# First stage of a one-core hybrid attention step: root, doubled rows, transposes, dummies and channel share changed

## The chip, the core and the metric

The kernel runs on one core of a Trainium2 chip. The metric is the device time of one execution, in microseconds (us). The engines are TensorE (PE for its matmuls, PEld for its weight loads), VectorE (DVE), ScalarE (ACT), GpSimd (POOL) and SyncE (SP, which issues most DMAs).

## What is computed

One layer of a decoder step, for 1024 prompt tokens and 8 sample tokens of width 1024. The input is normalised by its root mean square and multiplied with one combined weight; the columns of the result feed a gated short convolution and an attention with three branches (compressed, selected, window). Cut to what the change touches:

```
def rms_norm(x, g):
    xf = xf * lax.rsqrt(jnp.mean(xf * xf, axis=-1, keepdims=True) + NORM_EPS)
    return (xf * g.astype(jnp.float32)).astype(x.dtype)
...
    h = rms_norm(x, norm_g)
    proj = h @ w_in
    b_gate, c_gate, conv_in, z_conv, q, kv, gate_logits, z_attn = jnp.split(proj, offs, axis=-1)
    q = rope(rms_norm(q, q_gain), pos) * (HEAD_DIM ** -0.5)
    k = rope(rms_norm(kv[:, :, :, 0], k_gain[:, None, :]), pos)
...
    attn_branch = attn_o.reshape(bsz, t, ATTN_W) * jax.nn.silu(z_attn)
```

## The kernel before, in words

Every fp32 product is made of halves: an operand is split into a high part (a copy rounded to fp32r, on ACT) and a low part (the difference, on DVE or POOL), and three matmuls are added up in one PSUM bank. `w_loader` (L152) fetches weight pieces by DMA into `wraw` buffers and splits them into `wh` and `wl`; `wl0` serves the token products (256 or 280 columns, two `wraw` buffers), `w1` the channel products (128 weight columns).

The first stage is `phase0` (L519). It goes over 9 token tiles (8 of 128 prompt tokens, one of 8 sample tokens) five times, once per weight: the key/value rows of the compressed branch (`c0`), of the selected branch (`c1`), of the window branch (`c2`), and the queries in two halves. `tok_mm` (L193) makes one product of a tile: 24 matmuls into one of three `mm` banks.

`x_norm` (L368) prepares an input tile two tiles ahead: sum of squares on ACT, `rsqrt` (L180), scaling on DVE (L374), eight transposes on PE (L380), and the split into `hH` (ACT) and `hL` (DVE). `rsqrt` computes mean plus epsilon on DVE (L184), the root on ACT (L185), and four DVE instructions that take the reciprocal and mend it by one step. `norm_rope` (L245) does the same per head for key and query rows: squares (two heads by two ACT instructions with a running sum, L251; four heads by one ACT instruction and a DVE reduction, L253 and L254), `rsqrt`, and rope on DVE (L258 to L266).

Key rows must stand doubled before they are transposed. `twice` (L268) copies them on DVE into a `kd` tile; the tile for four rows shares one buffer with other small things (`CWR`), that for two rows has one buffer. `post` (L490) keeps the transposes that follow (`cmp_transposes` L390, `k_finish` L474) back by one step; `twice` is called there, together with them.

Beside `phase0` runs a second stream of products, `chan_stream` (L306): four weight columns of 128 for the attention's gate (`z_attn`), three products each (384, 384 and 264 tokens, 24 matmuls each, L215 to L217), copied into `mixA`. `merge` (L30) decides which stream goes next: always the one with the smaller ratio of work done to its weight, 150 for `phase0` and `ZW` = 31 for the channel stream; the numbers that the streams yield are their work. When both are done, one ACT instruction applies SiLU to the whole of `mixA` (L642), and attention begins; the later channel products belong to the convolution and fill attention's gaps.

The order on each engine is not that of the code: a scheduler sorts the recorded instructions, and each engine then takes them strictly in turn. So the printed order decides what queues behind what.

## Time and profile before

| | us |
|---|---|
| median of 3 runs (lowest, highest) | 952.64 (951.82, 954.2) |
| the profiled execution | 951.0 |
| its span, first to last instruction | 948.9 |
| PE busy | 876.9 (92%), 5765 matmuls |
| DVE busy | 612.6 (65%) |
| ACT busy | 556.1 (59%) |
| POOL busy | 404.1 (43%) |

The span is what the trace covers; the profiled execution is 2.1 us longer, the runs' median 1.6 us more than that. Times in the trace count from the start of the span. A busy PE can still be slow: its clock has two levels, 2.4 GHz (granted clock 1.00) and 1.2 GHz (0.50).

### The profile page before, as it was taken

The numbers are of one execution on the slowest core, as the hardware profiler recorded it, in microseconds if no ns is written. First come the engines' busy times: TensorE is split into PE (matmuls) and PEld (weight loads), VectorE is DVE, ScalarE is ACT, GpSimd is POOL, SyncE is SP. The second block draws the span as 40 slices with busy tenths as digits, with TensorE's granted clock in tenths as the row PEclk, the third lists the DMA queues.
The fourth block names the chain that finished last, engine by engine and source line by source line (L and its number), as shares of the span: only waits on it lengthen the run. The fifth ranks groups of instructions, "written<-read, shape, count | busy, mean of one in ns | idle before, by whom it ended". The sixth has DMA issues, their size and how long they took to land.

```text
span 948.9 us, 16963 instructions
## 1 busy us (share of the span) xinstructions
PE 876.9 (92%) x5765; PEld 787.1 (83%) x5765; DVE 612.6 (65%) x1744; ACT 556.1 (59%) x1489; POOL 404.1 (43%) x550
## 2 busy tenths in 40 slices
PE   5989889999999999999999999999779999798998
PEld 4878879899879889998998998999668888576765
DVE  3887656588456555567557558547845555777883
ACT  5754434533668667565656555555846766676761
POOL 4213322221366543444444443342364543467761
PEclk9999989999999999999999999999979999799999
DMA  6614230311000000000000000000477562847631
GB/s 220 176 35 114 65 121 24 90 56 31 23 24 22 13 12 23 23 23 23 25 23 23 23 23 23 22 2 1 118 260 264 188 203 82 309 148 252 202 110 46
DMA packets 57954, 82.23 MB, mean 87 GB/s; under 512 B 14470, under 2 KB 43086, under 8 KB 55692
## 3 DMA queue, kind: packets, MB, share of 16 engines
q1 hardware_dynamic: 50956, 47.60, 16.7%
q0 software_dynamic: 6912, 33.56, 10.5%
q8 instruction: 45, 0.74, 0.3%
q14 instruction: 41, 0.34, 0.1%
HBM read 74.24 MB, written 11.10 MB: 90 GB/s over the span
## 4 chain that ended last, share of the span: by engine, by line
PE 46%; DVE 6%; ACT 6%; issue 3%; DMA 2%; POOL 2%; SPq 0%; ACTq 0%; POOLq 0%; DVEq 0%
PE o L845 6%; PE mm L217 5%; PE mm L216 5%; PE mm L215 5%; PE s L762 5%; PE pt L836 4%; PE pt L956 1%; PE mm L1364 1%; PE mm L1362 1%; PE mm L1363 1%; PE o L1235 1%; PE om L980 1%; PE mm L980 1%; PE pt L1163 1%; ACT P L752 1%
## 5 line engine op out<-in xcount | busy, mean ns | idle before, releaser
L215 PE MATMUL mm<-hH,wh 128*128 128x384 f32 (+1 forms) x480 | 159.1, 331 | 0.0
L216 PE MATMUL mm<-hL,wh 128*128 128x384 f32 (+1 forms) x480 | 156.6, 326 | 0.0
L217 PE MATMUL mm<-hH,wl 128*128 128x384 f32 (+1 forms) x480 | 156.2, 326 | 0.2 <-POOL wl L78 0.2
L78 POOL TENSOR_TENSOR wl<-wraw,wh 128x256 fp32r<-128x256 f32 (+1 forms) x120 | 90.8, 774 | 120.4 <-ACT wh L74 89.7
L752 ACT ACTIVATE P<-P,stat 128x640 f32<-128x640 f32 (+7 forms) x192 | 113.0, 590 | 43.0 <-DVE stat L750 42.2
L78 DVE TENSOR_TENSOR pl<-pt,ph 128x512 fp32r<-128x512 f32 (+1 forms) x164 | 101.8, 634 | 45.6 <-ACT ph L74 44.6
L74 ACT ACTIVATE ph<-pt 128x512 fp32r<-128x512 f32 (+1 forms) x164 | 87.1, 547 | 57.5 <-PE pt L836 56.6
L811 POOL TENSOR_SCALAR P<-P,stat,gates 128x640 f32<-128x640 f32 (+7 forms) x128 | 101.3, 800 | 42.9 <-DVE stat L802 34.6
L836 PE MATMUL pt<-ident,P 128*128 128x128 f32 x592 | 93.3, 279 | 6.5 <-POOL P L811 2.1
L762 PE MATMUL s<-k,q 128*128 128x320 f32 (+8 forms) x416 | 96.4, 335 | 2.0 <-ACT q L74 1.9
L200 PE MATMUL mm<-wh,hH 128*128 128x256 f32 (+1 forms) x320 | 95.2, 299 | 2.9 <-ACT wh L74 1.9
L201 PE MATMUL mm<-wl,hH 128*128 128x256 f32 (+1 forms) x320 | 95.7, 299 | 1.5 <-POOL wl L78 1.0
L202 PE MATMUL mm<-wh,hL 128*128 128x256 f32 (+1 forms) x320 | 94.8, 297 | 0.4 <-DVE hL L78 0.2
L217 PEld LDWEIGHTS mm<-hH,wl 128*128 128x128 f32 x480 | 92.5, 193 | 0.6 <-POOL wl L78 0.5
L215 PEld LDWEIGHTS mm<-hH,wh 128*128 128x128 f32 x480 | 92.7, 193 | 0.3 <-ACT wh L74 0.2
L216 PEld LDWEIGHTS mm<-hL,wh 128*128 128x128 f32 x480 | 92.6, 193 | 0.1
L750 DVE CUSTOM_DVE_ANT_0 P<-s,mask 128x32 f32<-128x32 f32 (+8 forms) x160 | 69.8, 473 | 34.2 <-PE s L762 28.5
L836 PEld LDWEIGHTS pt<-ident,P 128*128 128x128 f32 x592 | 69.7, 141 | 18.1 <-POOL P L811 7.5
L845 PE MATMUL o<-pl,v 128*128 128x256 f32 x264 | 73.4, 300 | 5.6 <-DVE pl L78 5.4
L845 PE MATMUL o<-ph,v 128*128 128x256 f32 x264 | 74.8, 301 | 2.9 <-ACT ph L74 2.5
L762 PEld LDWEIGHTS s<-k,q 128*128 128x128 f32 x416 | 67.0, 191 | 5.8 <-ACT q L74 2.5
L807 POOL TENSOR_SCALAR P<-P,stat,gates 128x32 f32<-128x32 f32 x64 | 22.7, 367 | 108.5 <-DVE stat L802 97.4
(339 smaller groups left out, 2177.7 us busy)
## 6 DMA issues: line engine op xcount, KB each, us to landing
wraw<-in_w_in_dram SPq DMA_DIRECT2D x56, 256.0 KB
xt<-in_x_prompt_dram SPq DMA_DIRECT2D x8, 512.0 KB
wor<-in_w_out_dram SPq DMA_DIRECT2D x16, 256.0 KB
xr<-in_x_prompt_dram SPq DMA_DIRECT2D x16, 256.0 KB
out_y_prompt_dram<-xr SPq DMA_DIRECT2D x16, 256.0 KB
sd<-in_state_win_kv_dram SPq DMA_DIRECT2D x8, 512.0 KB
out_s_win_dram<-in_state_win_kv_dram SPq DMA_DIRECT2D x8, 511.0 KB
cwr<-in_cmp_w_dram SPq DMA_DIRECT2D x32, 64.0 KB
```

What stands on the lines that cost most here:

```text
L78: return eng.tensor_tensor(out, a, b, OP.subtract)
L200: PE.matmul(o[:, :n], hH[t // 3][:, k, s], wh, start=k == 0, stop=False)
L201: PE.matmul(o[:, :n], hH[t // 3][:, k, s], wl, start=False, stop=False)
L202: PE.matmul(o[:, :n], hL[t // 3][:, k, s], wh, start=False, stop=k == 7)
L215: PE.matmul(o[:, :n], wh, hH[c][:, k], start=k == 0, stop=False)
L216: PE.matmul(o[:, :n], wh, hL[c][:, k], start=False, stop=False)
L217: PE.matmul(o[:, :n], wl, hH[c][:, k], start=False, stop=k == 7)
L752: return lambda: ACT.activation(P, P, AF.Exp, bias=stt[:, 0, c:c + 1], scale=-1.0, accum_out=stt[:, 1, c:c + 1])
L762: PE.matmul(s[:, a:b], q[:, i], k, start=first, stop=not first)
L811: POOL.tensor_scalar(P[:, i, :n], P[:, i, :n], stt[:, 2, c + i:c + i + 1], gates[:, qi, gt:gt + 1], op0=OP.mult, op1=OP.mult)
L836: PE.transpose(p[:, y * 256 + i * 128:y * 256 + i * 128 + 128], src[:, i], ident)
L845: PE.matmul(o[0][:, :256], v, X[:, y * 256:y * 256 + 256], start=br == 1 and x == 0 and y == 0 and X is h[0], stop=last and y + 1 == len(p ...
```

## The change

- `rsqrt` takes the sum of squares already divided: ACT's square gets the scale 1/32 (inputs) or 1/8 (heads). The root is taken of the mean directly, with epsilon as the bias of the ACT instruction; the first DVE instruction (L184) goes. A root of a constant is issued at the start.
- The queries' sums come from four ACT squares per tile with running sums; the DVE reduction (L254) goes.
- 24 dummy matmuls with an operand of zeros are issued at the start. They write a bank that a later product overwrites.
- The third and fourth piece of the first weight get buffers of their own in the input tiles' pool.
- `x_norm` returns its transposes; they are called behind the next tile's product. `twice` is called as soon as the rows are made; `posted` lets the transposes follow after one step (`cmp_transposes`) or two (`k_finish`). The tile for two rows has three buffers instead of one, `rows` three instead of four.
- `ZW` goes from 31 to 55; SiLU on `mixA` is issued when the channel stream's four columns are done. The compression weight's split follows its fetch by one tile, and the second weight's splits follow their fetches by one tile.

```
+    WARM = 24
...
+    eps = cst.tile([128, 2], F32, name="eps")
+    DVE.memset(eps, EPS)
+    eps, root = eps[:, 0:1], eps[:, 1:2]
+    ACT.activation(root, eps, AF.Sqrt)
...
+    warm = ps.tile([128, 512], F32, name="cc", tag="cc", bufs=2)
+    for _ in range(WARM):
+        PE.matmul(warm[:, :256], vpc[:, 0], vpc.rearrange("p g c -> p (g c)"), start=True, stop=True)
...
+            def fetch(i, home=wp):
+                r = home.tile([128, kp, n], F32, name="wraw", bufs=raw_bufs)
                 SP.dma_start(r[:, :, :width], w_in[:, i * kp:(i + 1) * kp, col:col + width])
...
-    def rsqrt(wk, ss, n, c, scale):
-
-        t = wk.tile([128, 4, 8], F32, name="rs", bufs=4)
-        v, s, r, a = (t[:n, i, :c] for i in range(4))
-        DVE.tensor_scalar(v, ss, scale, EPS, op0=OP.mult, op1=OP.add)
-        ACT.activation(s, v, AF.Sqrt)
+    def rsqrt(wk, ss, n, c):
+
+        t = wk.tile([128, 3, 8], F32, name="rs", bufs=4)
+        s, r, a = (t[:n, i, :c] for i in range(3))
+        ACT.activation(s, ss, AF.Sqrt, bias=eps[:n])
         DVE.reciprocal(r, s)
-        DVE.tensor_tensor(a, v, r, OP.mult)
+        DVE.scalar_tensor_tensor(a, ss, EPS, r, op0=OP.add, op1=OP.mult)
         DVE.scalar_tensor_tensor(a, a, -0.5, r, op0=OP.mult, op1=OP.mult)
         DVE.scalar_tensor_tensor(r, a, 1.5, r, op0=OP.add, op1=OP.mult)
...
-        if nh == 2:
-            for h in range(2):
-                ACT.activation(sq[:n, h * 64:h * 64 + 64], src[:, h * 64:h * 64 + 64], AF.Square, accum_out=ss[:n, h:h + 1])
-        else:
-            ACT.activation(sq[:n, :w], src, AF.Square)
-            DVE.tensor_reduce(ss[:n, :nh], sq[:n, :w].rearrange("p (h d) -> p h d", h=nh), axis=AX, op=OP.add)
-        r = rsqrt(wk, ss[:n, :nh], n, nh, 1.0 / 64)
+        for h in range(nh):
+            c = slice(h * 64, h * 64 + 64)
+            ACT.activation(sq[:n, c], src[:, c], AF.Square, scale=0.125, accum_out=ss[:n, h:h + 1])
+        r = rsqrt(wk, ss[:n, :nh], n, nh)
...
-        kd = wk.tile([128, n, 2, 64], F32, name=f"kd{n}", tag="cwr" if n == 4 else "kd2", bufs=CWR if n == 4 else 1)
+        kd = wk.tile([128, n, 2, 64], F32, name=f"kd{n}", tag="cwr" if n == 4 else "kd2", bufs=CWR if n == 4 else 3)
...
-    LAG, DEPTH, HK, HB, XB, ZW, CWR = 1, 2, 2, 4, 3, 31.0, 1
+    LAG, DEPTH, HK, HB, XB, ZW, CWR = 1, 2, 2, 4, 3, 55.0, 1
...
-    ROWS, KLAG, CLAG = 4, 1, 1
+    ROWS = 3
...
     def x_norm(t):
...
-        ACT.activation(junk[:n], xt, AF.Square, accum_out=ss[:n])
-        r = rsqrt(wk, ss[:n], n, 1, 1.0 / D)
+        ACT.activation(junk[:n], xt, AF.Square, scale=1.0 / 32, accum_out=ss[:n])
+        r = rsqrt(wk, ss[:n], n, 1)
         DVE.scalar_tensor_tensor(xt, xt, r, gbc[:n], op0=OP.mult, op1=OP.mult)
-        for b in range(2):
...
+        def turn_x():
+            for b in range(2):
+                p = bank("tp")
...
+            seen[0] = t + 1
+        return turn_x
+
+    def cmp_transposes(kd, t):
+
...
-    def k_finish(br, t, rows2):
+    def k_finish(br, t, kds):

         p = bank("tp")
         pv = p.rearrange("p (g c) -> p g c", g=2)
         for i in range(2):
-            kd = twice(wk, rows2[i], 2)
             for g in range(2):
-                PE.transpose(pv[:, g, i * 128:i * 128 + 128], kd[:, g].rearrange("p r d -> p (r d)"), ident)
+                PE.transpose(pv[:, g, i * 128:i * 128 + 128], kds[i][:, g].rearrange("p r d -> p (r d)"), ident)
...
-    def post(fn, lag):
-
-        posts.append(fn)
-        while len(posts) > lag:
-            posts.pop(0)()
+    def posted(steps):
+
+        posts[:] = [(fn, n - steps) for fn, n in posts]
+        while posts and posts[0][1] <= 0:
+            posts.pop(0)[0]()

     def kv_tile(t, w, n, br, tab):
-        rows, _ = kv_rows(wk, tok_mm(t, w, n), t, br, *tab)
+        o = tok_mm(t, w, n)
+        posted(1)
+        rows, _ = kv_rows(wk, o, t, br, *tab)
         if t < 8:
             v = V[br][:, t]
             rv = rows[:, 128:256].rearrange("p (g d) -> p g d", g=2)
             copy(ACT, v[:, :, 0:64], rv)
             sub(POOL, v[:, :, 64:128], rv, f(v[:, :, 0:64]))
-            late[br].append(rows)
+            late[br].append(twice(wk, rows, 2))
         if t in (1, 3, 5, 7):
-            post(lambda r=late[br], t=t: k_finish(br, t - 1, r), KLAG)
+            posts.append((lambda r=late[br], t=t: k_finish(br, t - 1, r), 2))
             late[br] = []

...
+        posted(1)
...
         x_load(1)
-        c0[1](2)
+        c0[1](2, xsp)
+        c0[1](3, xsp)
         x_load(2)
         SP.dma_start(rope0, io["c_rope"])
-        x_norm(0)
+        turns = [x_norm(0)]
+        turns.pop(0)()
         tab0 = rope_tables(io["k_gain"][0, 0], 0, 1.0)
         for i in range(4):
             c0[2](i, *E0)
-            if i == 0:
-                c0[1](3)
         x_load(3)
-        x_norm(1)
+        turns.append(x_norm(1))
+        turns.pop(0)()
         c1 = wl0(COL_KV + 256, 256)
         for t in range(NT):
             if t + 4 < NT:
                 x_load(t + 4)
             if t + 2 < NT:
-                x_norm(t + 2)
-            rows, _ = kv_rows(wk, tok_mm(t, c0[0], 256), t, 0, *tab0)
+                turns.append(x_norm(t + 2))
+            o = tok_mm(t, c0[0], 256)
+            if turns:
+                turns.pop(0)()
+            posted(1)
+            rows, _ = kv_rows(wk, o, t, 0, *tab0)
             if t < 8:
-                post(lambda rows=rows, t=t: cmp_transposes(rows, t), CLAG)
+                posts.append((lambda kd=twice(wk, rows, 4), t=t: cmp_transposes(kd, t), 1))
             if t == 7:
                 tab1 = rope_tables(io["k_gain"][0, 1], 1, 1.0)
+            if t in (1, 2):
+                for i in (2 * t - 2, 2 * t - 1):
+                    c1[2](i)
             if t < 2:
                 for i in (2 * t, 2 * t + 1):
                     c1[1](i)
...
+        posted(9)
         xss.close()
         cw = xcp2.enter_context(pool("cw")).tile([128, 16, 2, 128], F32R, name="cw")
-        post(lambda: None, 0)
...
+            if 0 < t < 5:
+                cw_split()
             if t < 4:
-                cw_piece(wk, cw, t)
+                cw_split = cw_fetch(wk, cw, t)
             yield 3400
...
             yield next(chan)
+        ACT.activation(mAf, mAf, AF.Silu)

     merge((phase0(), 150.0), (z_part(), ZW))
-    ACT.activation(mAf, mAf, AF.Silu)
```

How the printed order moves, in three places. First PE, where the first weight's first products stand (`tp<-ident,xt` are the transposes of an input tile, `mm` the product). Before:

```order
L202 MATMUL mm_244<-wh_172,hL0_89 128x256
L200 MATMUL mm_244<-wh_176,hH0_88 128x256
L201 MATMUL mm_244<-wl_177,hH0_88 128x256
L380 MATMUL tp_204<-ident_58,xt_122 128x128 x4
L380 MATMUL tp_211<-ident_58,xt_122 128x128 x4
L202 MATMUL mm_244<-wh_176,hL0_89 128x256
L200 MATMUL mm_244<-wh_180,hH0_88 128x256
```

And after the change:

```order
L209 MATMUL mm_255<-wl_216,hH0_91 128x256
L210 MATMUL mm_255<-wh_215,hL0_92 128x256
L388 MATMUL tp_230<-ident_58,xt_150 128x128 x4
L388 MATMUL tp_237<-ident_58,xt_150 128x128 x4
L208 MATMUL mm_356<-wh_187,hH0_91 128x256
L209 MATMUL mm_356<-wl_188,hH0_91 128x256
L388 MATMUL tp_280<-ident_58,xt_156 128x128 x4
L388 MATMUL tp_287<-ident_58,xt_156 128x128 x4
```

The second tile's transposes stood in the middle of the first product and now follow it. At the very start of PE stand the 24 dummies. The first query product has six channel products ahead of it in PE's order before, and eleven after.

Second DVE, at key rows of the second weight (`ra`, `rb` and `rows` are a tile's rope, `kd2` its doubled rows, `rs` the steps of a root). Before:

```order
L261 TENSOR_TENSOR ra_1277<-qn_1275,mixC_72 128x128
L264 TENSOR_TENSOR rb_1278<-qn_1275,mixC_72 128x2x32 x2
L266 TENSOR_TENSOR rows_1262<-ra_1277,rb_1278 128x128
L75 COPY kd2_1357<-rows_1172 128x256
L184 TENSOR_SCALAR rs_1334<-ss_1331 128x2
L75 COPY kd2_1479<-rows_1262 128x256
```

After:

```order
L271 TENSOR_TENSOR rows_1245<-ra_1259,rb_1260 128x128
L76 COPY kd2_1268<-rows_1245 128x256
L194 RECIPROCAL rs_1308<-rs_1308 128x2
L195 SCALAR_TENSOR_TENSOR rs_1308<-ss_1305,rs_1308 128x2
L196 SCALAR_TENSOR_TENSOR rs_1308<-rs_1308 128x2
L197 SCALAR_TENSOR_TENSOR rs_1308<-rs_1308 128x2
```

The copy for a tile's rows (`rows_1172`) stood behind the whole rope of the next tile; it now stands right behind its own rows.

Third ACT, around SiLU (`mixA` holds the channel products; `q1`, `q3` to `q5` are copies of query tiles: before, attention's transposed ones, after, the first stage's). Before:

```order
L74 ACTIVATE mixA_73<-mm_3400 128x264
L642 ACT_TABLE_LOAD
L642 ACTIVATE mixA_73<-mixA_73 128x4128
L74 ACTIVATE q1_3489<-pt_3486 128x256
L74 ACTIVATE mixC_72<-mm_3509 128x384
```

After:

```order
L75 ACTIVATE mixA_76<-mm_2704 128x264
L75 ACTIVATE wh_2730<-wraw_2309 128x256
L75 ACTIVATE wh_2734<-wraw_2309 128x256
L656 ACT_TABLE_LOAD
L656 ACTIVATE mixA_76<-mixA_76 128x4128
L75 ACTIVATE q3_1873<-mm_2738 128x256
L75 ACTIVATE q4_1874<-mm_2784 128x256
L259 ACTIVATE sq_2764,ss_2765<-q3_1873 128x64 x4
L75 ACTIVATE q5_1875<-mm_2840 128x256
L193 ACT_TABLE_LOAD
L193 ACTIVATE rs_2770<-ss_2765,eps_61 128x4
```

SiLU stood ahead of attention's first query copy; it now stands among the query tiles of the first stage, with a table load of its own and one for the root behind it.

## Rows read from the trace of the kernel before

**Rows 1.** Windows: length, busy us (count) of five engines, clock, DMA share, GB/s.
```profile
9.20:72.20 63.00, 54.83 (x356) 50.84 (x357) 46.93 (x162) 37.38 (x119) 19.38 (x22) 0.92 0.41 125
72.20:169.40 97.20, 87.03 (x628) 83.63 (x626) 64.08 (x237) 42.28 (x182) 29.54 (x43) 0.93 0.29 84
169.40:244.60 75.20, 73.50 (x565) 72.01 (x564) 56.58 (x225) 30.54 (x93) 16.32 (x25) 1.00 0.17 49
244.60:256.20 11.60, 10.16 (x53) 9.37 (x52) 2.60 (x17) 10.10 (x20) 3.57 (x8) 0.85 0.18 46
123.90:129.30 5.40, 5.40 (x21) 5.40 (x22) 2.28 (x8) 2.22 (x9) 0.00 (x0) 0.50 0.43 128
85.60:88.60 3.00, 3.00 (x16) 3.00 (x16) 2.72 (x11) 0.95 (x4) 1.56 (x2) 0.50 0.65 171
```

**Rows 2.** Waits of PE to 253 us: waiter, releaser: sum, times, longest.
```profile
PE tp L380 <- DVE xt L374: 10.6, 3, 9.2
PE tp L481 <- DVE kd L75: 5.7, 3, 3.1
PE tp L591 <- DVE rs L184: 2.4, 1, 2.4
...
PE mm L200 <- ACT wh L74: 1.9, 1, 1.9
PE s L762 <- ACT q L74: 1.3, 1, 1.3
PE tp L444 <- POOL per L441: 1.2, 1, 1.2
```

**Rows 3.** Timeline of the first 14 us: start, duration, engine, instruction.
```profile
0.74 0.31 POOL L103 MEMSET vpc<- 128x256 f32 x1 [0.29 <-POOLq L1469]
...
5.56 1.28 ACT L185 ACT_TABLE_LOAD   x1
...
9.21 1.97 PE L380 MATMUL tp<-ident,xt 128*128 128x128 f32 x8 [9.21 <-DVE xt L374]
...
12.84 0.41 PE L201 MATMUL mm<-wl,hH 128*128 128x256 f32 x1
12.86 0.38 SPq L160 DMA_DIRECT2D wraw<-in_w_in_dram  x1
...
13.48 0.41 PE L201 MATMUL mm<-wl,hH 128*128 128x256 f32 x1
```

**Rows 4.** Groups by form, DVE, to 252 us: busy, mean ns, idle before.
```profile
L254 DVE TENSOR_REDUCE ss<-sq 128x4 f32<-128x256 f32 x16 | 6.6, 412 | 8.2 <-ACT sq L253 8.2
...
L184 DVE TENSOR_SCALAR rs<-ss 128x2 f32<-128x2 f32 x24 | 4.6, 193 | 10.6 <-ACT sq L251 10.5
```

**Rows 5.** The same for ACT.
```profile
L251 ACT ACTIVATE sq<-rows 128x64 f32<-128x64 f32 x48 | 11.9, 248 | 1.3 <-POOL per L441 0.9
L251 ACT ACTIVATION_READ_ACCUMULATOR sq<-rows 128x1 f32 x48 | 9.0, 187 | 0.0
...
L253 ACT ACTIVATE sq<-q 128x256 f32<-128x256 f32 x16 | 6.7, 416 | 0.7 <-DVE rs L188 0.3
```

**Rows 6.** Timeline of PE in the second weight's products.
```profile
72.21 0.28 PE L200 MATMUL mm<-wh,hH 128*128 128x256 f32 x1
...
73.28 0.28 PE L200 MATMUL mm<-wh,hH 128*128 128x256 f32 x1
```

**Rows 7.** Timeline of POOL and DVE around 204 and 217 us.
```profile
204.20 3.39 POOL L78 TENSOR_TENSOR wl<-wraw,wh 128x256 fp32r<-128x256 f32 x4 [17.19 <-PE mm L205]
204.54 1.58 DVE L264 TENSOR_TENSOR rb<-qn,mixC 128x128 f32<-128x128 f32 x2
...
217.03 0.48 DVE L264 TENSOR_TENSOR rb<-qn,mixC 128x128 f32<-128x128 f32 x2
```

**Rows 8.** Timeline of ACT at SiLU.
```profile
245.45 1.28 ACT L642 ACT_TABLE_LOAD   x1
246.74 3.65 ACT L642 ACTIVATE mixA<-mixA 128x4128 f32<-128x4128 f32 x1
```

More of the change, by code (lines that the diff above doesn't have):

```diff
@@ L156, in load @@
             hs, ls, raws = [], [], []
-            def fetch(i):
-                r = wp.tile([128, kp, n], F32, name="wraw", bufs=raw_bufs)
+            def fetch(i, home=wp):
+                r = home.tile([128, kp, n], F32, name="wraw", bufs=raw_bufs)
                 SP.dma_start(r[:, :, :width], w_in[:, i * kp:(i + 1) * kp, col:col + width])
@@ L371, in x_norm @@
         ss = wk.tile([128, 1], F32, name="xss", bufs=3)
-        ACT.activation(junk[:n], xt, AF.Square, accum_out=ss[:n])
-        r = rsqrt(wk, ss[:n], n, 1, 1.0 / D)
+        ACT.activation(junk[:n], xt, AF.Square, scale=1.0 / 32, accum_out=ss[:n])
+        r = rsqrt(wk, ss[:n], n, 1)
         DVE.scalar_tensor_tensor(xt, xt, r, gbc[:n], op0=OP.mult, op1=OP.mult)
-        for b in range(2):
-            p = bank("tp")
-            pv = p.rearrange("p (k c) -> p k c", k=4)[:, :, :n]
-            for k in range(4):
-                kk = b * 4 + k
-                PE.transpose(pv[:, k], xt[:, kk * 128:(kk + 1) * 128], ident[:n, :n])
-            o = slice(t % 3 * 128, t % 3 * 128 + n)
-            dh, dl = (x[t // 3][:, b * 4:b * 4 + 4, o] for x in (hH, hL))
-            copy(ACT, dh, pv)
-            sub(DVE, dl, pv, f(dh))
-            if t == 8:
-                copy(DVE, hS[:, b * 4:b * 4 + 4, 0:8], f(dh))
-                copy(DVE, hS[:, b * 4:b * 4 + 4, 32:40], f(dl))
-        seen[0] = t + 1
-    def cmp_transposes(rows, t):
-        kd = twice(wk, rows, 4)
+        def turn_x():
+            for b in range(2):
+                p = bank("tp")
+                pv = p.rearrange("p (k c) -> p k c", k=4)[:, :, :n]
+                for k in range(4):
+                    kk = b * 4 + k
+                    PE.transpose(pv[:, k], xt[:, kk * 128:(kk + 1) * 128], ident[:n, :n])
+                o = slice(t % 3 * 128, t % 3 * 128 + n)
+                dh, dl = (x[t // 3][:, b * 4:b * 4 + 4, o] for x in (hH, hL))
+                copy(ACT, dh, pv)
+                sub(DVE, dl, pv, f(dh))
+                if t == 8:
+                    copy(DVE, hS[:, b * 4:b * 4 + 4, 0:8], f(dh))
+                    copy(DVE, hS[:, b * 4:b * 4 + 4, 32:40], f(dl))
+            seen[0] = t + 1
+        return turn_x
+    def cmp_transposes(kd, t):
         p = bank("tp")
@@ L404, in hymba_step_kernel @@
     cmpw = io["cmp_w"]
-    def cw_piece(wpool, cw, i):
-        cw_fetch(wpool, cw, i)()
     def cw_fetch(wpool, cw, i):
@@ L551, in phase0 @@
                     c1[1](i)
-                    c1[2](i)
             yield 3900
+        posted(9)
         xss.close()
         cw = xcp2.enter_context(pool("cw")).tile([128, 16, 2, 128], F32R, name="cw")
-        post(lambda: None, 0)
         c2 = wl0(COL_KV + 512, 280)
@@ L567, in phase0 @@
                 c2[1](t // 2 + 1)
+            if 0 < t < 5:
+                cw_split()
             if t < 4:
-                cw_piece(wk, cw, t)
+                cw_split = cw_fetch(wk, cw, t)
             yield 3400
-        post(lambda: None, 0)
+        posted(9)
         kc = wk.tile([128, 2, 2, 33], F32, name="kc")
@@ L616, in phase0 @@
             yield 3600
-        post(lambda: None, 0)
+        posted(9)
         ACT.activation(gates[:, 0:8], gates[:, 0:8], AF.Sigmoid)
```

## The prediction

> **What bounds the kernel now.** I read the page first: TensorE (PE) is busy 92% of the span, no other engine more than 65%. So time can come back only where PE stands or runs slowly. The stretches come next [rows 1]. I cut the first stage (everything before attention) where PE goes from one kind of product to the next: A, the products of the first key/value weight (9.2 to 72.2 us); B, the other two key/value weights (72.2 to 169.4); C, the queries (169.4 to 244.6); D, the way into attention (244.6 to 256.2). PE is idle for 63.0 - 54.8 = 8.2 us in A, 97.2 - 87.0 = 10.2 in B, 75.2 - 73.5 = 1.7 in C and 1.4 in D, and it does nothing before 9.2. The granted clock takes more: its mean is 0.92 in A and 0.93 in B, so 8% of 63.0 = 5.0 us and 7% of 97.2 = 6.8 us are lost to the lower level. The two short stretches in [rows 1] at 0.50, the 1.2 GHz level, show it bare: one begins as a wait for doubled key rows ends, the other follows a wait of 1.2 us. C has the mean 1.00, and PE is full there.
>
> What PE waited for [rows 2]: 9.2 us for the first scaled input tile, then mostly DVE: 5.7 us in three waits for the doubled key rows, 2.4 for the compressed keys; 1.9 for a weight half from ACT, 1.2 for a small POOL copy, and 1.3 at attention's first score.
>
> **The change, part by part.** A product of 24 matmuls with 256 columns takes 24 x 0.119 = 2.9 us at full clock: nine matmuls lie between the starts 72.21 and 73.28 [rows 6]. A channel product with 384 columns is then 24 x 0.119 x 384/256 = 4.3, one with 264 columns 2.9, both worked out from the columns.
>
> Start. Before the first root ACT loads a table for 1.28 us [rows 3], between the sum of squares and the root on which all else hangs. The new root of a constant pulls that load into the time in which ACT waits for the input. That gains 1.3 us. The dummies are 24 matmuls at the slow spacing, (13.48 - 12.84)/3 = 0.213 us [rows 3], so 5.1 us, from 0.74 + 0.31 = 1.05 on, when the memset of their operand is over. They end near 6.2 and PE is first wanted near 7.9: they cost nothing. Without that cover each would cost its 0.2. If they raise the clock, the first product could gain 24 x (0.213 - 0.119) = 2.3 us; but its low weight halves come from POOL one by one at about 0.85 each (four in 3.39, [rows 7]), 7 us for eight. So I take 0, and keep 2.3 as an end.
>
> The fourth weight piece was issued only at 12.86 [rows 3], for it waited for a buffer, and PE then waited 1.9 for it [rows 2]. With its own buffers it is issued at the start. The input tile that it overtakes on SP's queue is the third, needed later. The loads of rope and gains stay behind it.
>
> Roots. Each of them loses one DVE instruction, 0.19 us [rows 4]. In A there are 17 (9 inputs, 8 row tiles): 3.3 us at most. DVE is busy 46.9 of A's 63.0 us, with what it waits for in between, so I take it as the wall of A and count 2 of the 3.3. For queries the reduction goes too: 16 x (0.41 + 0.16) = 9.1 us of DVE in C, at a price on ACT: four squares with their reads, at most 4 x (0.25 + 0.19) = 1.8 us, for one of 0.42 [rows 4, 5]. That is at most 1.4 x 18 = 25 us on ACT, which is busy 30.5 of C's 75.2; the rest covers it. Were it not covered, C would get up to its 25 us longer; it is not near.
>
> Filler. By the printed order, eleven of the twelve channel products stand ahead of the first query product, where before there were six. One more (2.9 us) lies in A, four in B. A product moved into a stand is free; one moved into full PE time only changes place. A's moved product I count in full, 2.9, since DVE sets A. A: 1.3 + 2 + 2.9 = 6, between 0 (DVE and PE wait for each other as before) and 12 (half of its idle and clock losses gone as well).
>
> B. Doubled rows are now made right behind their row tile and transposed two steps later, so the 5.7 us of waits go, with the 2.7 us that the slow stretch of 5.4 us behind one of them cost [rows 1, 2]. The POOL copy's transposes move behind more products: 1.0 of 1.2, and 1.5 of the slow 3.0 us. That is 10.9. What is late next is the compressed keys' chain (2.4 us [rows 2]), which I leave in, with its slow spell. Of the remaining 17.0 - 10.9 = 6.1 us I let the four extra fillers take 1. B: 12, between 7 (only waits that are named, half of the clock's part) and 16.
>
> C. Five products leave it, so four of 4.3 us and one of 2.9, so PE needs 75.2 - 20.1 = 55.1 us. DVE needs 56.6 - 9.1 = 47.5. PE still sets it: 0. Here SiLU now falls. On ACT it is 1.28 + 3.65 us [rows 8], and the root's table comes back for another 1.28: 6.2 us in which no product is copied out. PE has three banks, 3 x 2.9 = 8.7 us of products, so it is hidden; what is queued behind it on ACT (copies, squares, weight halves) slips by as much. The next instruction on ACT starts 1.29 us after the table load does [rows 8]. The Trainium skill (ScalarE: Activation LUTs, What ACT_TABLE_LOAD costs) speaks against placing it there: it puts a switch of sets at about 2.66 us, load and drain together. By that price the block is 3.65 + 2 x 2.66 = 9.0 us, 0.3 over the 8.7, and the sum 0.3 us worse; the row shows no drain in that place.
>
> D. Attention's first query split stood behind SiLU. With ACT free the wait of 1.3 us goes [rows 2]; I take 1.5, between 0 and 3.
>
> **Sum**: 6 + 12 + 0 + 1.5 = 19.5 off the profiled execution's 951.0 us gives 931.5. The median of the runs, 952.64, lies 1.6 above that execution, so I predict **933 us**. The later stages are PE-bound on the whole and I let them carry the gain through.
>
> **Rivals.**
> - DVE stays the wall. Two more weight columns are split before C, 8 POOL instructions at 0.85. While POOL splits, a pair of DVE multiplies takes 1.58 us, otherwise 0.48 [rows 7]. For it: DVE sets A already. Against it: in B it is busy only 64.1 of 97.2. The Trainium skill (Perfetto Trace Analysis, Optimizing Scalar/DVE Operations) states that the two engines share a read port; the rows agree. Then A keeps its 1.3 and B 7: 951.0 - 8.3 + 1.6 = 944.
> - Everything closes: A 12, B 16, D 3, so 31 us, and 922. For it: more fillers and a steady PE at the 2.4 GHz level. Against: the compressed keys' chain is untouched.
> - Slower. The doubled rows of stretch A have one buffer. DVE's copy for a tile waits for PE's transposes of the tile before, which now stand behind a whole product and the transposes of an input that DVE must first scale. If the two engines go in lockstep, DVE stands for a product and its transposes at each of 8 tiles: 2.9 us, and for the twelve transposes 1.5, an estimate from eight that took 1.97 at the lower level [rows 3]. That is 8 x 4.4 = 35 us, of which the 16 that DVE idles in A now are paid already. 19 more against 13.5 gained in B and D: 952.6 + 5.5 = 958. It decides from 13.5 us in A on. Against it: the buffer is single today too, and those transposes stand well ahead of the next copy.
> - No difference. The doubled rows weren't what PE waited for, or C without its fillers opens as many stands as A and B close: 952.
>
> **Chances.** My forecast 0.63, DVE as the wall 0.15, everything closes 0.14, slower 0.04, no difference 0.04. About 0.3% (2.9 us) is what a measurement of this kernel can tell from no change. So faster 0.92, same 0.04, slower 0.04. The range takes in the first rival and the second, with the loose ends of A: 917 to 945.
>
> **What would show it.** PE's first transposes near 7.9 us; no wait of a us or more for doubled rows; the first query product near 171 us, about where it is today, but with eleven channel products done, 20 us of work more; SiLU on ACT in the middle of the queries with PE full beside it; PE's last first-stage product near 226. Wrong, if the mean clock in A and B does not rise above 0.95, if a stand of 2 us or more opens in C, or if PE waits for DVE's copies in A for more than 3 us.

## The result, and the profile after

| | before | after |
|---|---|---|
| median of 4 runs each (lowest, highest), us | 953.27 (951.82, 954.2) | 942.74 (942.33, 946.37) |
| ratio, 95% interval | | 0.9909 [0.9887, 0.9932] |
| profiled execution, us | 951.0 | 942.42 |
| its span, us | 948.9 | 940.6 |
| PE busy, us | 876.9 (92%) | 875.1 (93%) |
| DVE, ACT, POOL busy, us | 612.6, 556.1, 404.1 | 607.7, 569.9, 403.2 |

Faster by some 9 us, where 19.5 were forecast: the ratio gives 8.7, the two profiled executions 8.6, the two medians 10.5. 942.74 lies inside the range that was given, but by the ratio and the profiles the gain is less than half of what the sum said, so the sum has to be taken apart.

The same four stretches as in [rows 1], in the windows of the changed kernel (length, then busy us and count of PE, PEld, DVE, ACT and POOL, the granted clock, DMA share, GB/s). They are cut at first transposes, first product of the second weight, first query product, last product of the first stage, and attention's first output. All but the last are the events of [rows 1], whose last stretch ends at 256.2, 1.5 us ahead of attention's first output there (257.7).

```profile
8.03:75.51 67.48, 56.28 (x380) 52.77 (x381) 49.34 (x145) 40.27 (x124) 20.24 (x24) 0.87 0.39 126
75.51:178.66 103.15, 98.97 (x726) 96.09 (x724) 62.87 (x231) 48.14 (x198) 32.19 (x46) 0.98 0.35 95
178.66:237.61 58.95, 56.20 (x444) 54.29 (x443) 44.99 (x155) 40.40 (x195) 12.09 (x16) 0.97 0.14 37
237.61:250.06 12.45, 11.29 (x65) 9.62 (x64) 8.11 (x41) 7.45 (x29) 4.73 (x12) 1.00 0.05 13
```

A's clock fell from 0.92 to 0.87 and its idle PE time rose from 8.2 to 67.48 - 56.28 = 11.2 us. B went from 0.93 to 0.98. C, with 1.7 us of idle PE and the clock 1.00 before, now has 2.75 us and 0.97.

The stretches hold different numbers of channel products, so their lengths can't be compared directly. I compare **at equal work**: from the time at which a token product ends, take 0.119 us for every 256 columns of every channel matmul done by then (a column of three products is 11.5 us by that). The 9th token product, the last of the first weight, ended at 72.4 with 8.6 us of channel work before (63.8) and at 75.7 with 11.5 after (64.2), so A gained -0.4. The 27th, the last before the queries, stands at 10.9 us ahead, the 45th, the last of the first stage, at 7.4 (233.50 - 34.54 = 198.96 against 237.61 - 46.05 = 191.56). Attention's first output came 257.7 - 250.06 = 7.7 us earlier, and the end 8.3.

| stage | forecast | measured, equal work |
|---|---|---|
| A | 6 | -0.4 |
| B | 12 | 10.9 + 0.4 = 11.3 |
| C | 0 | 7.4 - 10.9 = -3.5 |
| D | 1.5 | 7.7 - 7.4 = 0.3 |
| behind it | 0 | 8.3 - 7.7 = 0.6 |

The waits of PE up to 238 us (waiter, releaser, us in total, times, longest) show what is left. They answer to [rows 2]:

```profile
PE tp L388 <- DVE xt L380: 5.4, 4, 2.0
PE tp L388 <- DVE rs L196: 3.5, 1, 3.5
PE mm L208 <- ACT wh L75: 2.3, 3, 1.2
PE tp L388 <- DVE rs L194: 2.0, 1, 2.0
PE mm L209 <- POOL wl L79: 1.7, 6, 0.5
PE mm L224 <- DVE hL L79: 1.5, 1, 1.5
...
PE tp L607 <- DVE kc L602: 0.7, 1, 0.7
PE tp L485 <- DVE kd L76: 0.7, 1, 0.7
```

The waits for doubled key rows (5.7 us) and the 2.4 us for the compressed keys are down to 0.7 each. PE now waits most for input tiles: 10.9 us, 2.0 of them ahead of A for the first tile, and the longest of them, 3.5, in A. In PE's timeline this is the place, in A:

```profile
62.29 0.63 PE L388 MATMUL tp<-ident,xt 8*128 8x8 f32 x8 [3.48 <-DVE rs L196]
62.84 0.83 PE L404 MATMUL tp<-ident,kd 128*128 128x128 f32 x4
63.32 0.57 PE L223 MATMUL mm<-hH,wh 128*128 128x264 f32 x1
65.39 0.59 PE L224 MATMUL mm<-hL,wh 128*128 128x264 f32 x1 [1.51 <-DVE hL L79]
```

and the window of the channel product that follows, down to its end:

```profile
63.32:70.52 7.20, 5.69 (x28) 5.39 (x27) 4.33 (x15) 2.03 (x6) 3.77 (x5) 0.53 0.06 20
```

PE stands 3.48 us for the last input tile (8 rows), another 1.51 for its low half, and the channel product, with that second stand in it, takes 7.20 us at the clock 0.53 where 2.9 are due at full clock. That is 3.5 + 4.3 = 7.8 us at one place: 5.0 of standing and 2.8 of slow clock.

### The profile page after: what moved, and what is told of

It reads as the page before. It is cut to its first block, busy times and chain, and to the rows that moved or that the text cites. A ratio compares the mean times of both kernels' runs of the same rounds, so it can differ in the third digit from the quotient of the medians.

```text
span 940.6 us, 17090 instructions
## 1 busy us (share of the span) xinstructions
PE 875.1 (93%) x5789; PEld 785.4 (84%) x5789; DVE 607.7 (65%) x1673; ACT 569.9 (61%) x1616; POOL 403.2 (43%) x550
## 4 chain that ended last, share of the span: by engine, by line
PE 46%; DVE 7%; ACT 6%; issue 4%; POOL 2%; DMA 1%; ACTq 0%; DVEq 0%; POOLq 0%
PE o L861 6%; PE mm L225 5%; PE mm L224 5%; PE pt L852 5%; PE mm L223 5%; PE s L778 4%; PE mm L1380 1%; ACT P L768 1%; PE pt L972 1%; PE mm L1379 1%; PE mm L1378 1%; PE o L1251 1%; PE om L996 1%; PE mm L996 1%; PE om L1378 1%
## 5 line engine op out<-in xcount | busy, mean ns | idle before, releaser
L79 POOL TENSOR_TENSOR wl<-wraw,wh 128x256 fp32r<-128x256 f32 (+1 forms) x120 | 88.2, 752 | 111.9 <-ACT wh L75 89.2
L210 PE MATMUL mm<-wh,hL 128*128 128x256 f32 (+1 forms) x320 | 92.8, 291 | 0.0
```

What stands on the lines that cost most here:

```text
L79: return eng.tensor_tensor(out, a, b, OP.subtract)
L210: PE.matmul(o[:, :n], hL[t // 3][:, k, s], wh, start=False, stop=k == 7)
```

## The experiments

Each is the changed kernel with one edit or two, or once more as it is (e15). The last four columns give the gain on the kernel before at the 9th, 27th and 45th token product (at equal work) and at attention's first output (in plain time), from one profiled execution of each. Ratios are whole runs against the kernel before on the same chip; the medians come from several chips, so the ratios are what compares.

| run | median us | ratio, interval | 9th | 27th | 45th | output |
|---|---|---|---|---|---|---|
| the change | 942.74 | 0.9909 [0.9887, 0.9932] | -0.4 | 10.9 | 7.4 | 7.7 |
| e1_turn_now | 943.65 | 0.9920 [0.9896, 0.9945] | -1.2 | 9.3 | 6.1 | 6.3 |
| e2_turn_lag2 | 946.5 | 0.9956 [0.9937, 0.9974] | 2.2 | 6.4 | 3.0 | 3.2 |
| e3_kd_late | 949.09 | 0.9978 [0.9956, 1.0001] | 0.7 | 7.2 | 5.9 | 3.8 |
| e4_zw31 | 943.39 | 0.9920 [0.9902, 0.9939] | 4.4 | 7.7 | 9.1 | 9.1 |
| e5_hold_a | 943.99 | 0.9904 [0.9866, 0.9942] | 3.1 | 6.8 | 7.0 | 7.3 |
| e6_hold_c | 939.11 | 0.9877 [0.9821, 0.9932] | -0.8 | 10.6 | 9.8 | 10.1 |
| e7_hold_ac | 944.02 | 0.9903 [0.9871, 0.9936] | 3.5 | 8.6 | 6.6 | 6.8 |
| e8_no_dummies | 940.48 | 0.9861 [0.9820, 0.9903] | -1.8 | 9.7 | 9.2 | 9.5 |
| e9_no_low_split | 944.74, one run | | 0.5 | 11.1 | 7.7 | 7.9 |
| e10_roots_old | 948.28 | 0.9965 [0.9951, 0.9980] | -2.3 | 5.9 | 1.8 | 0.9 |
| e11_silu_late | 939.66 | 0.9870 [0.9840, 0.9901] | -0.4 | 11.1 | 9.1 | 9.4 |
| e12_hold_ac_share65 | 947.02 | 0.9967 [0.9938, 0.9996] | 4.4 | 10.8 | 4.5 | 4.7 |
| e13_last_tile_late | 947.21 | 0.9948 [0.9934, 0.9962] | 0.2 | 5.7 | 3.4 | 3.7 |
| e14_last_tile_hold_c | 944.55 | 0.9934 [0.9910, 0.9957] | 1.7 | 6.2 | 6.9 | 7.1 |
| e15_after_again | 943.33 | 0.9905 [0.9873, 0.9938] | -0.5 | 10.8 | 8.8 | 9.0 |
| e16_hold_c_again | 939.65 | 0.9882 [0.9860, 0.9904] | -0.5 | 11.5 | 10.6 | 10.9 |

Executions with the same order of instructions differ, too. The changed kernel's order ran three times (the first row, e11 and e15): by 0.1 us at the 9th product, 0.3 at the 27th, 1.7 at the 45th. e6 and e16, also one order, differ by 0.3, 0.9 and 0.8. And the table ends at attention's first output: behind it the profiled executions lose up to 4 us or gain as many (e10 goes from 0.9 to -3.2 at the end of its span, e14 from 7.1 to 11.2), so the whole time doesn't follow from the first stage alone. e10's profiled execution (953.9 us) is the slowest of its ten, e14's (939.8) the fastest of its seven.

**Where do the input tiles' transposes belong?** e1 records them ahead of the product again:

```
-                turns.append(x_norm(t + 2))
+                x_norm(t + 2)()
             o = tok_mm(t, c0[0], 256)
-            if turns:
-                turns.pop(0)()
```

> The changed kernel with one part undone: an input tile's transposes are recorded ahead of the product again, as in the kernel before. Theory L (the input chain's lead): stage A missed its 6 us because the transposes now stand right behind one product, where the chain of square, root and scaling has one product's time; that gave the stands of 2.0 us at 34.9, 3.5 us at 58.8 and 1.5 us at 63.9 and the slow clock behind them. Then A gets 4 to 6 us shorter here and the time is 937 to 940 us. Rival D (DVE is the wall of A whatever the order): the stands change place, A stays within 1 us and the time is 942 to 945 us.

A did not get shorter (9th product 0.8 us later). The waits came back at the same places, 3.02 us for the last tile among them. Theory L fell in this form: recorded ahead of the product or behind it, the chain that makes the tile ends after that product. e2 puts them one product later still:

```
-            if turns:
+            if len(turns) > 1 or (turns and t > 6):
                 turns.pop(0)()
```

> The changed kernel with the input tiles' transposes one product later still. Theory L: the waits of PE for scaled input tiles (10.9 us in the changed kernel up to 65 us, the first 2.0 of them at the start) fall under 5 us, A gets 4 to 6 us shorter, and the time is 936 to 939 us. Rival D: DVE sets the pace, PE waits for it elsewhere in A, and the time stays within 942 to 945 us.

Here A gained 2.6 us on the changed kernel, less than the 4 to 6 of L, and the run was slower: B lost it again. At 117.7 us PE stood 2.9 us for doubled rows and ran slowly behind that.

**What did B win by?** e3 makes the doubled rows of the later weights late:

```
-            late[br].append(twice(wk, rows, 2))
+            late[br].append(rows)
...
-            posts.append((lambda r=late[br], t=t: k_finish(br, t - 1, r), 2))
+            posts.append((lambda r=late[br], t=t: k_finish(br, t - 1, r), 1))
...
+            kd = twice(wk, kds[i], 2)
...
-        kd = wk.tile([128, n, 2, 64], F32, name=f"kd{n}", tag="cwr" if n == 4 else "kd2", bufs=CWR if n == 4 else 3)
+        kd = wk.tile([128, n, 2, 64], F32, name=f"kd{n}", tag="cwr" if n == 4 else "kd2", bufs=CWR if n == 4 else 1)
```

(and `rows` with four buffers again)

> The changed kernel with the doubled rows of the second and third weight made late again, right ahead of their transposes, one step later, with one buffer. Theory K (as in the prediction): B won its 10.9 us because these copies no longer stand behind the next tile's rope; then waits of 2 to 3 us for the doubled rows come back, B gets 6 to 10 us longer and the time is 948 to 953 us. Rival F (the four extra channel products closed B): B gets under 3 us longer, 943 to 946 us.

The waits came back, here in PE's waits up to 238 us:

```profile
PE tp L486 <- DVE kd L76: 4.0, 3, 2.1
...
PE tp L486 <- DVE rs L194: 1.4, 1, 1.4
```

From the 9th to the 27th product B gained 7.2 - 0.7 = 6.5 us instead of 11.3, so 4.8 of it was the doubled rows: the time, 949.09, is as theory K says, the loss in B somewhat below its 6 to 10. e4 takes the fillers back:

```
-    LAG, DEPTH, HK, HB, XB, ZW, CWR = 1, 2, 2, 4, 3, 55.0, 1
+    LAG, DEPTH, HK, HB, XB, ZW, CWR = 1, 2, 2, 4, 3, 31.0, 1
```

> The changed kernel with the channel share back at 31, so six channel products ahead of the queries instead of eleven. Theory K: B keeps most of its gain, C gets its fillers back and loses the stands at the second query weight (about 3.7 us with the slow clock behind them), so 939 to 943 us. Rival F: without the fillers B loses 5 us or more, 945 to 950 us.

Each theory had a part of this. B gained only 7.7 - 4.4 = 3.3 us, so without the extra fillers 8.0 of its 11.3 were gone: a wait of 2.0 us for doubled rows and one of 2.4 for the compressed keys, both followed by stretches at 0.73 and 0.61. C ended 1.4 us up instead of 3.5 down, as K says. And A, of which neither spoke, went from -0.4 to 4.4. PE's waits for input tiles no longer have the 3.5, and the clock stays up:

```profile
PE tp L388 <- DVE xt L380: 5.5, 4, 2.2
PE tp L485 <- DVE kd L76: 2.4, 2, 2.0
PE tp L607 <- DVE kc L602: 2.4, 1, 2.4
PE tp L388 <- DVE rs L194: 2.1, 1, 2.1
```

```profile
60.00:75.00 15.00, 12.56 (x106) 11.78 (x106) 11.07 (x31) 6.29 (x22) 6.41 (x7) 1.00 0.19 51
```

The order fits. At share 31 the second channel product stands behind the seventh token product, ahead of the last input tile's transposes. At 55 it is spent two token products earlier, and the third can't cover that wait: its 264 tokens include the last tile's.

**Fillers held back.** e5, e6 and e7 hold channel products at named places:

```
+        hold, n = {1: ("c0", 6), 11: ("q", 0, 7)}, 0
         while "z" not in done:
-            yield next(chan)
+            while n in hold and hold[n] not in done:
+                yield None
+            c = next(chan)
+            n += c is not None
+            yield c
```

e7 is shown; e5 has only the first entry, e6 only the second. `done` is set by `phase0` behind the seventh product of the first weight, and behind the eighth query product.

> The changed kernel, but the second channel product is held back until the seventh product of the first weight is recorded, so that it stands ahead of the last input tile's transposes. Theory S (a share spent too early): A missed its 6 us because the second channel product was spent ahead of the sixth token product, and the third can't cover the wait for the last input tile, since it needs that tile itself. Then the stand of 3.5 us at 58.8 and the slow clock of 63 to 70 go, and the ninth token product of the first weight ends 4 to 5 us earlier at equal work; if B keeps its gain, 938 to 940 us. Rival D (DVE is the wall): the stand moves elsewhere in A, under 1 us, 942 to 944 us.

> The changed kernel, but the last channel product is held back until the first query weight's eight full products are recorded, so that it stands where the second query weight is still being split. Theory W (C lacks a filler at that place): the waits of 0.5 and 0.9 us at 209 to 214 and the slow clock of 216 to 219 go, C gets 3 to 3.5 us shorter, and the time is 939 to 940 us. Rival M (the product only changes place, and SiLU, now later, holds ACT there): C stays within 1 us, 942 to 944 us.

> Both holds together. Theories S and W: the gains add up, 4 to 5 us in A and 3 to 3.5 in C, and the time is 934 to 937 us. If stands move instead (D, M), 941 to 944 us.

A: theory S is shown, with somewhat less than its 4 to 5 us. The 9th product came 3.5 and 3.9 us earlier than in the changed kernel. What is left of the stand, in e7's timeline:

```profile
64.79 0.28 PE L212 MATMUL mm<-wh,hS 128*40 128x256 f32 x1 [1.40 <-DVE hS L76]
```

The clock doesn't recover in full: over 63 to 72 us of e7 it is 0.81. And B gave the gain back. In e7, PE's waits to 238 us and the window behind the longest of them:

```profile
PE tp L485 <- DVE kd L76: 3.1, 1, 3.1
PE tp L404 <- DVE kd L76: 2.3, 2, 1.8
```

```profile
118.15:128.00 9.85, 9.85 (x47) 9.85 (x47) 5.27 (x13) 3.57 (x11) 4.82 (x4) 0.50 0.51 135
```

The held products moved the sixth channel product, and with it the split of the next column, behind the second weight's last full product; in the changed kernel both are done before that product ends. In the timeline of e7, POOL's row and the rope of the last full key rows beside it:

```profile
112.73 5.21 POOL L79 TENSOR_TENSOR wl<-wraw,wh 128x256 fp32r<-128x256 f32 x7
```

```profile
114.99 1.52 DVE L269 TENSOR_TENSOR rb<-qn,mixC 128x64 f32<-128x64 f32 x2
```

In the changed kernel the pair of multiplies of the same rows, with POOL idle beside it, takes

```profile
119.69 0.35 DVE L269 TENSOR_TENSOR rb<-qn,mixC 128x64 f32<-128x64 f32 x2
```

From the root's reciprocal (111.71) to the end of the doubled copy (118.10) these rows took 6.4 us in e7, the rows before them 2.3 (108.26 to 110.59). Seven splits in a row made the doubled rows late, PE stood 3.1 us, and 9.85 us at the clock 0.50 followed. The Trainium skill (Perfetto Trace Analysis, Optimizing Scalar/DVE Operations) says that GpSimd and VectorE share a read port of SBUF; the rows agree with it. What a filler is worth can't be told from the filler alone: it brings its column's splits along.

The same exchange runs through the whole table. All six runs that gained 1.7 us or more up to the 9th product (e2, e4, e5, e7, e12, e14) gained only 3.3 to 6.4 in B, and in each PE stood 2.0 to 3.1 us for doubled rows at the end of the second weight. No run brought the 27th product more than 11.5 us ahead. Only in e7 is the cause followed up here; whether the order alone or DVE's pace ties A's gain to B's loss in the others, no run separates.

C: with the hold alone (e6) most of the waits at the second query weight is gone. PE's waits from 192 to 238 us, in e15 (the changed kernel's second run; its longest here are 0.51 and 0.91 us) and then in e6:

```profile
PE mm L209 <- POOL wl L79: 0.9, 3, 0.5
PE mm L208 <- ACT wh L75: 0.9, 1, 0.9
```

```profile
PE mm L209 <- POOL wl L79: 0.4, 2, 0.2
```

The same window in e6, in e15 and in the changed kernel's first profile:

```profile
205.00:220.00 15.00, 14.30 (x108) 12.90 (x107) 9.98 (x25) 14.43 (x45) 7.51 (x10) 1.00 0.19 54
```

```profile
205.00:220.00 15.00, 12.90 (x98) 11.65 (x98) 14.52 (x53) 10.20 (x59) 4.80 (x6) 1.00 0.20 54
```

```profile
205.00:220.00 15.00, 12.92 (x87) 11.67 (x86) 14.52 (x52) 10.07 (x58) 4.77 (x6) 0.89 0.19 54
```

PE is 14.30 us busy in these 15 instead of 12.9. From the 27th to the 45th product e6 lost 0.8 us, the changed kernel 3.5. So W is shown, but for its size: the slow clock belongs to the first profile. e15 and e11, the same order, have the same waits and stay at 1.00; each lost 2.0 in C (10.8 - 8.8, 11.1 - 9.1).

**The dummies.**

```
-    WARM = 24
+    WARM = 0
```

> The changed kernel without the 24 dummies at the start. The prediction's step (the dummies cost nothing and bring nothing): the first product ends within 0.5 us of where it ends now and the time stays within 1 us. Rival (they raise the clock for the first products): the first and second product run at the lower level for longer, 2 us or more later at equal work, 944 to 946 us.

The first product ended 3.0 us ahead of the kernel before at equal work, with the dummies 3.1. They are the row

```profile
1.11 4.91 PE L149 MATMUL cc<-vpc 128*128 128x256 f32 x24 [1.11 <-POOL vpc L104]
```

and PE's own first transposes come 2.0 us after its end. For the first product nothing was gained and nothing lost, as forecast. The 9th product stands 1.0 to 1.4 us later than in the five executions that have the changed kernel's order in A (-0.4 to -0.8), but without the dummies the scheduler set another order in A, so this isn't shown to be theirs. The ratio, 0.9861, can't be told from the changed kernel's 0.9870 to 0.9909: what the dummies do to the whole time stays open.

**The start.** e9 leaves out the first weight's low halves on POOL:

```
-                    sub(el, l[:, :, :width], r, f(h[:, :, :width]))
+                    if el is None:
+                        l = h
+                    else:
+                        sub(el, l[:, :, :width], r, f(h[:, :, :width]))
...
-    E0 = (ACT, POOL)
+    E0 = (ACT, None)
```

> The changed kernel without the eight low-half splits of the first weight on POOL: its products take the high half in their place, so the number of matmuls is the same and the compressed branch's rows lose their low part. Theory P (POOL's splits slow DVE at the start): beside them the second input tile's scaling took 2.40 us against 1.28 and two root steps 0.66 against 0.16, so PE stands 1.95 us at 15.3 and 1.14 at 19.2 and runs slowly after. Then both stands shrink below 1 us each, and the third token product ends 3 us or more earlier at equal work. Rival Q (the input tiles come late by DMA and ACT's order): the stands stay, the third product ends within 1 us of the changed kernel's.

The third product came 1.7 us earlier than in the changed kernel at equal work, between the two theories, and the stands stayed (1.59 and 1.19 us). The timeline shows why P can't be read clean. The two root steps went back from 0.66 to 0.16 us, but the splits were not what stood beside the scaling. In the changed kernel that was POOL's two rope table products,

```profile
14.65 3.77 POOL L246 TENSOR_TENSOR mixC<-mixC,g 128x576 f32<-128x576 f32 x2
```

```profile
14.76 2.40 DVE L380 SCALAR_TENSOR_TENSOR xt<-xt,rs,mixC 128x1024 f32<-128x1024 f32 x1
```

and e9 leaves them where they were:

```profile
14.26 1.41 POOL L249 TENSOR_TENSOR mixC<-mixC,g 128x576 f32<-128x576 f32 x1 [12.90 <-DMA g<-in_k_gain_dram]
```

```profile
14.27 2.48 DVE L383 SCALAR_TENSOR_TENSOR xt<-xt,rs,mixC 128x1024 f32<-128x1024 f32 x1
```

So the second input tile's scaling took 2.48 us all the same, and the third's, with POOL idle, 1.28 in both runs. PE's stand for the second tile ends with this scaling; by these durations some 1.1 us of its 1.95 are the collision with the rope table products, an estimate. By the ninth product 0.9 us of the gain were left.

**Roots and SiLU.**

```
-        ACT.activation(s, ss, AF.Sqrt, bias=eps[:n])
+        DVE.tensor_scalar(v, ss, 1.0, EPS, op0=OP.mult, op1=OP.add)
+        ACT.activation(s, v, AF.Sqrt)
...
+            ACT.activation(sq[:n, :w], src, AF.Square, scale=0.125)
+            DVE.tensor_reduce(ss[:n, :nh], sq[:n, :w].rearrange("p (h d) -> p h d", h=nh), axis=AX, op=OP.add)
```

(queries only for the second piece)

> The changed kernel with the roots as before (mean and epsilon by a DVE instruction) and the queries' sums by a DVE reduction again. The prediction counts 2 us for the roots in A and nothing in C: then A ends 2 us later at equal work, C stays, and the time is 944 to 946 us. Rival (the roots gain nothing, DVE isn't what PE waits for at most of them): within 1 us at every stage.

A ended 1.9 us later than in the changed kernel, the 2 us of the forecast. But the 27th product stands at 5.9 instead of 10.9: another 3 us went in B, 4.1 in C (5.9 - 1.8, the changed kernel 2.0 to 3.5), and the ratio is 0.9965. The roots were worth more than was counted; where, one profile, the slowest of ten executions, says only roughly.

```
             yield next(chan)
-        ACT.activation(mAf, mAf, AF.Silu)
...
+    ACT.activation(mAf, mAf, AF.Silu)
```

> The changed kernel with SiLU behind both streams again. The prediction counts 1.5 us for its move: then the wait of 1.3 us at attention's first score comes back, attention's first outputs come 1 to 2 us later, and C, with no six-microsecond block on ACT, stays within 0.5 us. Rival (SiLU's block on ACT makes the stands at the second query weight): C gets 2 us or more shorter.

This run tested nothing: the scheduler set the same order on all five engines. SiLU still began at 195.4 us:

```profile
L658 ACT ACTIVATE mixA<-mixA x1: 3662/3662/3662, 195.4 to 195.4; 128x4128 f32<-128x4128 f32 x1
```

In e4, with the line but share 31, SiLU begins at 237.6. So it is the channel share that moved SiLU, not the line, and e11 is a third run of the changed kernel: with it and e15 the change stands at 0.9909, 0.9905 and 0.9870.

**Both holds with the later products moved back, and the last tile by itself.**

```
-    LAG, DEPTH, HK, HB, XB, ZW, CWR = 1, 2, 2, 4, 3, 55.0, 1
+    LAG, DEPTH, HK, HB, XB, ZW, CWR = 1, 2, 2, 4, 3, 65.0, 1
```

> Both holds with the channel share at 65, which brings the later channel products back to nearly the places that they have in the changed kernel. In the run with both holds at share 55, B lost what A had won: seven POOL splits in a row at 112.7 to 117.9 slowed the last rope and copy of the second weight, PE stood 3.1 us for its doubled rows and ran at the lower level for ten more. If that collision is a matter of place: it goes, A keeps its 3.5 to 4 us and C its 2.4, and the time is 934 to 937 us. If another stand takes its place in B, 940 to 944 us.

The collision in B moved (a wait of 2.2 us at 111.7), A and B together kept 10.8, and the queries lost 6.3: ACT stood at a weight piece that was fetched late, with the query copies behind it and PE 3.1 us behind those.

```profile
192.15 0.42 ACT L75 ACTIVATE wh<-wraw 128x256 fp32r<-128x256 f32 x1 [5.58 <-DMA wraw<-in_w_in_dram]
```

```
-            if turns:
+            if turns and t != 6:
                 turns.pop(0)()
```

> The changed kernel, but the last input tile's transposes (8 rows, which the eighth token product doesn't need) stand behind the eighth token product instead of the seventh. Theory T (A's gain is lost in the wait for the last input tile and the slow clock behind it): the stand of 3.5 us goes, the clock stays up at 60 to 70 us, the ninth token product ends 2.5 to 4.5 us earlier at equal work, and the time is 2 to 4 us below the changed kernel's on this chip. Rival D (DVE is behind anyway): the wait moves to the low halves or the doubled rows, A stays within 1 us.

> The last input tile's transposes late, and the last channel product held back for the second query weight. Theories T and W: both gains stand, A 2.5 to 4.5 us and C 1 to 3.5, and the time is 5 us or more below the changed kernel's on this chip, 935 to 938 us. Rival: one of them is lost in B again, within 2 us of the hold in C alone.

The stand of 3.5 us went, as T says, but a stand of 2.9 us for the last tile's low half came in its place (e13 at 64.1, e14 at 63.8), so A gained only 0.6 and 2.1 us on the changed kernel. And B gained 5.5 and 4.5 instead of 11.3: a wait of 2.8 and 2.3 us at 123.4 for doubled rows, and ten us at 0.58 and 0.65 behind it. e13 and e14 have the same edit in A and still differ there by 1.5 us. On the same chip e13 came out slower than the changed kernel (0.9948 against 0.9905) and e14 not faster; the rival of e14, that a gain is lost in B again, is what came.

> The changed kernel once more, on the chip of these four: 940 to 943 us. The stands in A and C come at the same places; whether the slow clock follows the waits at the second query weight is open, in two runs of the same order there it did not.

> The hold in C once more: theory W expects 1 to 3.5 us below the changed kernel on this chip; rival M the same time within 1 us.

On this chip the hold in C had 939.65 (939.01 to 942.88, 6 runs), the changed kernel 943.33 (939.15 to 945.31, 4 runs). The hold came out at 0.9877 and 0.9882, the changed kernel's order at 0.9909, 0.9905 and 0.9870. At equal work it saves the 1.1 to 1.2 us between C's losses of 2.0 (e11, e15) and 0.8 or 0.9 (e6, e16). That it beats the kernel before is shown; that it beats the changed kernel is not settled, for e11's 0.9870 is as low as the hold's.

## Why the prediction was wrong

**A failed, and most of the miss is here.** "A's moved product I count in full, 2.9, since DVE sets A" was the wrong step. The product was not moved into a stand; a product that covered one was taken away. The extra share spent the second channel product two token products earlier, and the third depends on the very tile that PE waits for. With the share alone set back (e4) A gained 4.4 of the 6; the difference is 4.8 us, and with the second product alone held back it is 3.5 and 3.9 (e5, e7), so the term had the wrong sign. The stand was in the waits of the kernel before, in the part of the view that [rows 2] leaves out, and the working doesn't name it:

```profile
PE mm L204 <- DVE hS L75: 2.2, 1, 2.2
```

That is PE waiting for the last input tile, with the second channel product still ahead of it. The start was right: first transposes at 8.03 for the forecast 7.9, and the fourth weight piece no longer holds the first product, which ended 3.1 us ahead. But that was lost by the third product. There PE waits for input tiles; some 1.1 us of it is DVE's scaling beside POOL's rope table products (2.40 us against 1.28), the rest the runs don't separate. The 2 us for the roots were right (1.9 in e10).

**B was right in size (11.3 for 12), in part by luck, for its parts were wrong.** I gave the doubled rows and their clock most of the 10.9 and the fillers 1. Taking the fillers away cost 8.0, taking the early doubled rows away 4.8, the roots 11.3 - 8.2 = 3.1. They sum to more than the whole, so they aren't separate shares: the runs fit stands that more than one of them can close. And e4 reaches B 4.8 us earlier, so its 8.0 need not be the fillers' alone. The compressed keys' chain, which I left in with 2.4 us, fell to 0.7 because a channel product now stands there.

**C failed.** "PE still sets it: 0" looked at SiLU and the three banks, and those held: SiLU ran beside full PE. What I didn't ask is which stands the six channel products in C had covered. One of them stood between the two query weights, while ACT and POOL split the second one. With all twelve spent by 192 us PE waits there, 0.5 and 0.9 us and in small pieces between: 2.0 us, 3.5 with the slow clock of the first profile. The rival "C without its fillers opens as many stands as A and B close" had the mechanism, with far too much of it; the forecast gave it no us.

The table switch beside SiLU cost what the row before said, not more:

```profile
194.39 1.28 ACT L656 ACT_TABLE_LOAD   x1
195.69 3.66 ACT L656 ACTIVATE mixA<-mixA 128x4128 f32<-128x4128 f32 x1
```

The next instruction starts 1.30 us after the load starts. The Trainium skill (ScalarE: Activation LUTs, What ACT_TABLE_LOAD costs) states about 2.66 us for a switch, load and drain together; the row decides, and it shows 1.30.

**D** was small: the wait of 1.3 us at the first score is gone, but attention's first output is only 0.3 us further ahead than the first stage's end. **Behind it** the gain was carried through in this profile, as assumed: 7.7 us at attention's first output, 8.3 at the end. In the other two executions of this order it was 9.4 and 9.0, and 7.6 and 7.1 at the end.

Of the rivals, "DVE stays the wall" gave 944 and was nearest the time, for another reason: B gained all that was forecast. "Slower" did not come: PE's waits for doubled rows in A stay under 1 us. By the signs that I named, the clock in B (0.98) was right, A's (0.87) was below the 0.95 that I had called wrong, and the first query product at 178.66 and the last first-stage product at 237.6 were late by 8 and 12 us.

## What to carry to other kernels

Work that fills gaps is a fixed budget. Before you count a filler as gained where it goes, list the stand that it covers where it comes from, and check that it doesn't depend on what is being waited for. Price a stand of some us together with the clock behind it, and expect a fix in one stage to move splits and loads into the next one: only the whole run tells.

## What was not expected of the hardware

The clock behind a stand can cost more than the stand. In the changed kernel 3.48 + 1.51 us of standing went with 2.8 us of slow clock; in e7 3.1 us were followed by 9.85 at 0.50, half of which, 4.9, is lost. It isn't tied to the program alone: the same order with the same waits of 0.5 and 0.9 us ran on at 0.89 over 205 to 220 us in one profile and at 1.00 in two others. What decides between the two stays open.
